# Exchanging even and odd chunks in the second RWKV head pair, so that the two pairs' recurrence products lie on opposite halves of the array, and copying z and U with two engines

## The chip, the cores and the metric

The kernel runs on one core of a Trainium2 chip. The metric is the device time of one execution in microseconds; for several runs of one kernel the median is given. TensorE (PE) multiplies; VectorE (DVE), ScalarE (ACT) and GpSimd (POOL) do the rest of the arithmetic; SyncE (SP) only issues DMA transfers here. Each engine takes its instructions in the order in which they are written and waits on semaphores for the others.

## The reference, cut to what matters

Two layers of a decoder trunk, 512 tokens, width 1024, batch 1, all in float32. Each layer adds three sub-layers to the residual: a token mixer, a cross-attention into 256 memory tokens, and a SwiGLU feed-forward network. The mixer projects its normalised input once, gives the columns to four groups of heads, and multiplies their joined outputs by `w_out`.

```python
y = concatenate([rglru_group(p_a, ...), retention_group(p_b, ...),
                 rwkv7_group(p_c, ...), ssd_group(p_d, ...)])
x = x + y @ w_out[l]
x = x + memory_cross_attention(...)
x = x + swiglu(...)
```

The change lies in the RWKV-7 group, which has 4 heads of 64 channels and a state of 64 x 64 for each head. Token by token it is

```python
def step(state, inp):                   # state (heads, v, k)
    r_t, w_t, k_t, v_t, kk_t, a_t = inp
    sa = einsum('bhvk,bhk->bhv', state, -kk_t)
    state = (state * w_t[:, :, None, :] + sa[..., None] * (kk_t * a_t)[:, :, None, :]
             + v_t[..., None] * k_t[:, :, None, :])
    return state, einsum('bhvk,bhk->bhv', state, r_t)
```

## The kernel before, in words

**A planner sets the order.** The kernel doesn't write its instructions straight into the program. Every operation is recorded as an `Op` with an engine, an estimated duration from `cost()` (line 376) and its dependences (`record()`, line 302). `order()` (line 428) then builds a list schedule: at each turn it takes, over all engines, the operation that can start first by these estimates; among equals of one engine it looks at a class (dense projection passes yield to group work), at whether TensorE would have to change its tile shape, and at the length of the path behind the operation. `issue()` (line 552) writes the operations in that order, so every instruction of the trace has line 564, and a group of instructions is known by its tiles. A name such as `b<-z,s 64*64 64x64` means: output in a tile of kind b, weights from a tile of kind z, data from a tile of kind s, weights of 64 rows by 64 columns, output of 64 x 64. The kinds are pools: `a` and `b` are PSUM banks (a for dense projections, b for the rest), `s` are 512 columns of SBUF, `q` 128 columns, `z` 256 columns, `t` small vectors, `u`, `v` and `w` the stages of a weight block.

**Dense projections.** A weight block of 1024 x 128 is loaded by DMA to `u`, cast by ScalarE to its high part `v` (a CAST of 128 x 1024), and VectorE subtracts to get the low part `w`. Three passes over 512 tokens (`a<-s,v`, `a<-s,v`, `a<-s,w`) make one product in split precision. These passes are most of TensorE's work, and the planner lays the small products of the four groups between them. A product of plain float32 operands shows as two passes in the trace, each with its own weight load.

**RWKV, prepared by `rwkv_pair` (line 1126).** Two heads make a pair (i = 0, 1) of 128 channels. The 512 tokens are 8 chunks of 64. Chunks 2q and 2q + 1 share a block of 128 token rows, so an even chunk (e = 0) and an odd one (e = 1) lie in different 64-row halves. `ar` holds four slots of 64 columns for each q: y, z, z, y (`a4[:, :, 1:3]` is for z, `a4[:, :, 0:4:3]` for y); `bk` holds the keys in the same manner. Their products, multiplied by the triangular mask `rwa`, are the tiles `at[hf, o]` (half of the sequence hf, head o of the pair). Their inner 128 columns go to a scratch `nd` in DRAM, 4 DMAs for each pair (line 1195).

**The solve, `rwkv_solve` (line 1212).** GpSimd inverts the unit triangles in blocks of 32, all chunks and heads side by side: `n<-nd` brings them in, 62 products and sums follow, and the results go out to scratch (`fd<-s`, `fd<-n`) and come back as tiles (`s<-fd`, 16 DMAs for each of two results). `rwkv_whole` (line 1260) then merges the blocks of 32 into inverses of 64: 16 products, a masked copy by VectorE (two `s<-b,cst` operations), 16 products more. Its products are the `b<-s,s 64*64` passes; neighbouring ones take e = 0 and e = 1 in turn, which are the two diagonal quarters of the array.

**The recurrence, `rwkv_scan` (line 1282).** Eight steps c, one for each chunk. In each step, for both pairs and both heads (`po`, four products in a group):

- z: `zb[rw, oc(i, o)] += at[...][:, zcol].T @ u` (weights 128 x 64), behind the product with the state `st[i]`; `z` is copied out of PSUM by VectorE (64 x 256);
- U: `ub[rw, oc(i, o)] = Rs[i].T-product with z` (`b<-z,s 64*64`), copied to `u` by ScalarE (64 x 256);
- the new state: one full product for each pair, two operations on VectorE;
- y: `zb[ry, oc(i, o)] += at[...][:, ycol].T @ u` (weights 128 x 64), copied by ScalarE.

`rw` and `ry` are the two halves of the 128 rows, and both are set by e alone, so both pairs use the same half in a step. The order within a group is that of `po`, with i outside and o inside.

**Retention** shares VectorE and SP with it at that time. For each of four tiles it copies a projection, shifts it by 32 partitions with four DMAs (`s<-s`, 32 x 512), and multiplies the result by the rotary table (`s<-s,s` of 128 x 512, two operations in sequence).

Of the kernel before, what the change touches and what calls it, by code (L numbers as in the profile page):

```python
# [13 lines left out]
AF = mybir.ActivationFunctionType  # L14
ALU = mybir.AluOpType
# [68 lines left out]
def _constants():  # L84
# [25 lines left out]
    blocks["retg"] = g  # L110

    s = np.arange(HD)
    lt, le = s[:, None] < s[None, :], s[:, None] <= s[None, :]
    am = np.concatenate([le, lt, lt, le], 1)
    blocks["rwa"] = np.concatenate([am, am], 0).astype(np.float64)
    m = (s[:, None] // 32 == 1) & (s[None, :] // 32 == 0)
# [136 lines left out]
class Engine:  # L253
# [9 lines left out]
KINDS = {"s": (T, 71), "n": (1024, 1), "z": (256, 2), "t": (16, 64), "q": (P, 10), "u": (KD * P + 16, 3), "v": (KD * P + 16, 3), "w": (KD * P + 16, 3),  # L263
         "a": (T, 3), "b": (T, 5)}


class Sched:
# [108 lines left out]
    def cost(self, op, fn, out, ins):  # L376
# [12 lines left out]
        elif op.eng == "PE":  # L389
            op.lat = 200.0  # L390
            if fn == "transpose":
                op.dur = 85.0
                op.grid = "T"
            else:
                k, m, w = ins[0].shape[0], _free(ins[0]), _free(ins[1])
                op.grid = HD if k <= HD else P, HD if m <= HD else P
                if ins[0].ap.dtype == F32R:
                    op.dur = max(111.0, 6 + 0.4405 * w)
                else:

# [166 lines left out]
class Trunk:  # L567
# [558 lines left out]
    def rwkv_pair(self, l, i, lora, wa, k, r, v, nd):  # L1126
# [30 lines left out]
        V.tensor_tensor(k2, k2, k, op=ALU.mult)  # L1157
        ar, bk = {}, {}
        for hf in range(2):
            ar[hf] = self.S()  # L1160
# [5 lines left out]

            V.tensor_tensor(a4[:, :, 1:3, 1:], q4(kk)[:, :, :, 1:], q4(wi)[:, :, :, :HD - 1], op=ALU.mult)
            V.tensor_copy(a4[:, :, 1:3, 0:1], q4(kk)[:, :, :, 0:1])
            V.tensor_tensor(a4[:, :, 0:4:3], q4(r), q4(wi), op=ALU.mult)

            V.tensor_tensor(b4[:, :, 0:4:3], q4(k2), q4(wv), op=ALU.mult)
        wend = self.tiny()[:, :8]
        V.tensor_copy(wend, wi[:, HD - 1:T:HD])
        V.scalar_tensor_tensor(kk, kk, -0.5, wv, op0=ALU.mult, op1=ALU.mult)
        for hf in range(2):
            ts_ = slice(hf * 256, (hf + 1) * 256)
            q3 = lambda x: x[:, ts_].rearrange("p (q t) -> p q t", q=2)
            V.scalar_tensor_tensor(bk[hf].rearrange("p (q x) -> p q x", q=2)[:, :, HD:3 * HD], q3(ta), 1.0, q3(kk),
                                   op0=ALU.add, op1=ALU.mult)

        am = self.con("rwa")
        at, bt = {}, {}
        for hf in range(2):
            for o in range(2):
# [9 lines left out]
                n0 = 8 * i + 4 * hf + 2 * o  # L1194
                self.Q.dma_start(nd[:, n0:n0 + 2], t.rearrange("p (q x) -> p q x", q=2)[:, :, HD:3 * HD])

# [7 lines left out]
        for hf in range(2):  # L1204
# [3 lines left out]
            bt[hf] = self.S()  # L1208
            A.copy(bt[hf], b)
        return ar, at, bt, wend, k2, kk, v  # L1210

# [47 lines left out]

    def rwkv_whole(self, RT, at):  # L1260

# [4 lines left out]
        col = lambda c: slice((4 * c[0] + 2 * c[1] + c[2]) * HD, (4 * c[0] + 2 * c[1] + c[2] + 1) * HD)  # L1266
        zcol = lambda q, e: slice(q * 2 * P + (1 + e) * HD, q * 2 * P + (2 + e) * HD)
        b = self.bank()
        for c in cells:
            E.matmul(b[rows(c[3]), col(c)], at[c[0], c[1]][rows(c[3]), zcol(c[2], c[3])], TT[rows(c[3]), col(c)], start=True, stop=True)  # L1270
        x = self.S()
# [10 lines left out]
    def rwkv_scan(self, l, pairs, RT):  # L1282
# [4 lines left out]
        rows = self.rows  # L1287
        zcol = lambda q, e: slice(q * 2 * P + (1 + e) * HD, q * 2 * P + (2 + e) * HD)
        ycol = lambda q, e: slice(q * 2 * P + 3 * e * HD, q * 2 * P + (3 * e + 1) * HD)

        uv = {}
        for hf in range(2):
# [4 lines left out]
            for i in range(2):  # L1297
# [4 lines left out]
                for e in range(2):  # L1302
                    rw = rows(1 - e)
                    A.copy(uv[hf, e][rw, i], b[rw, 0:256].rearrange("p (q x) -> p q x", q=2))
        Rs = [self.rwkv_whole(RT[i], pairs[i][1]) for i in range(2)]
        st = [None, None]
        yt = [p[5] for p in pairs]
        for c in range(8):
            hf, qq, e, q = c // 4, c % 4 // 2, c % 2, c // 2
            rw, ry = rows(e), rows(1 - e)  # L1310
            ccol = slice((c % 4) * P, (c % 4 + 1) * P)
            u = uv[hf, e][:, :, qq]
            z = self.s.tile("z")
            zb, ub = self.bank(), self.bank()
            oc = lambda i, o: slice(i * P + o * HD, i * P + (o + 1) * HD)
            po = [(i, o) for i in range(2) for o in range(2)]
            if c:
# [20 lines left out]
            for i, o in po:  # L1338
                E.matmul(zb[ry, oc(i, o)], pairs[i][1][hf, o][:, ycol(qq, e)], u[:, i, o * HD:(o + 1) * HD], start=(c == 0), stop=True, skip_group_check=True)
            for i in range(2):  # L1340
                A.copy(yt[i][ry, q * P:(q + 1) * P], zb[ry, i * P:(i + 1) * P])
        for i in range(2):
# [3 lines left out]
            for j in range(4):  # L1346
                E.transpose(b[:, j * P:(j + 1) * P], y[:, j * P:(j + 1) * P], ident)
            A.activation(y, b, AF.Identity, bias=self.par("rwkv_gn_b", l, i), scale=self.par("rwkv_gn_w", l, i))
            V.tensor_tensor(y, y, pairs[i][4], op=ALU.add)
# [364 lines left out]
```

## Time and profile before

| | |
|---|---|
| median of 3 runs | 1683.56 us (1681.34 to 1685.95) |
| profiled execution | 1683.98 us, span 1682.1 us |
| granted clock of TensorE, mean | 0.992 of full speed |
| TensorE busy | 1643.6 us (98%), 8344 passes |
| VectorE busy | 1015.1 us (60%), 1796 instructions |
| ScalarE busy | 633.2 us (38%), 966 instructions |
| GpSimd busy | 69.6 us (4%), 140 instructions |
| the chain that ended last | TensorE 91%, VectorE 4%, DMA 2%, ScalarE 2% |

The span is the profiler's view of one execution; the time is measured around it. Busy is the time in which an engine executes something, and passes of TensorE that overlap count once. The recurrence of the first layer runs from about 174 to 242 us, that of the second from about 1000 to 1060.

### The profile page before, as it was taken

How to read it: one execution, taken by the hardware profiler on the slowest of the kernel's cores; microseconds unless marked ns; L12 is line 12 of the kernel's file. 1: busy time of each engine (PE TensorE's matmuls, PEld its weight loads, DVE VectorE, ACT ScalarE, POOL GpSimd, SP SyncE). 2: the span in 40 equal slices, each digit the busy share in tenths (PEclk: the TensorE clock that was granted, in tenths of full speed). 3: DMA queues.
4: the chain of work that ended last, by engine and by line, in shares of the span. 5: the costliest groups of instructions: out<-in, count | busy, mean ns of one | idle time of the engine just before them, and what ended most of it. 6: DMA issues, size and time to landing. Idle time of an engine off the chain costs nothing.

```text
span 1682.1 us, 21417 instructions
## 1 busy us (share of the span) xinstructions
PE 1643.6 (98%) x8344; PEld 1344.0 (80%) x8344; DVE 1015.1 (60%) x1796; ACT 633.2 (38%) x966; POOL 69.6 (4%) x140
## 2 busy tenths in 40 slices
PE   7998999999999999999999989999999999999997
PEld 7786778888788888888888867888888888888886
DVE  8867689666564545533477666986655655554333
ACT  7433246444442322322354332554444323232221
POOL 0043000000000000000000700000000000000001
PEclk9999999999999999999999999999999999999998
DMA  9345112632323333333453431145233333333331
GB/s 287 103 101 126 26 45 81 189 94 66 97 88 99 89 100 90 95 104 114 131 175 101 107 83 45 51 126 162 64 88 88 100 89 99 93 96 94 92 97 57
DMA packets 312900, 169.48 MB, mean 101 GB/s; under 512 B 35936, under 2 KB 300384, under 8 KB 312672
## 3 DMA queue, kind: packets, MB, share of 16 engines
q1 hardware_dynamic: 312800, 168.12, 34.8%
q8 instruction: 66, 1.08, 0.3%
q14 instruction: 34, 0.28, 0.1%
HBM read 156.56 MB, written 9.44 MB: 99 GB/s over the span
## 4 chain that ended last, share of the span: by engine, by line
PE 91%; DVE 4%; DMA 2%; ACT 2%; SPq 1%; issue 1%; DVEq 0%; ACTq 0%
PE a L564 81%; PE b L564 9%; DVE s L564 2%; ACT s L564 1%; DMA s<-s 1%; DVE w L564 1%; SPq L564 1%; ACT v L564 1%; DMA s<-in_lora_dram 0%; DMA s<-fd 0%; DMA s<-in_memT_dram 0%; DVE q L564 0%; DVE t L564 0%; DVEq L1710 0%; DVE z L564 0%
## 5 line engine op out<-in xcount | busy, mean ns | idle before, releaser
L564 PE MATMUL a<-s,v 128*128 128x512 f32 (+1 forms) x4012 | 1234.0, 388 | 7.6 <-ACT s L564 5.9
L564 PEld LDWEIGHTS a<-s,v 128*128 128x128 f32 x4012 | 743.8, 189 | 168.2 <-ACT s L564 6.5
L564 PE MATMUL a<-s,w 128*128 128x512 f32 (+1 forms) x2006 | 777.2, 387 | 0.5 <-DVE w L564 0.5
L564 ACT CAST v<-u 128x1024 fp32r<-128x1024 f32 (+3 forms) x275 | 282.4, 1027 | 673.6 <-PE a L564 384.4
L564 PEld LDWEIGHTS a<-s,w 128*128 128x128 f32 x2006 | 378.8, 189 | 80.0 <-issue 0.9
L564 DVE TENSOR_TENSOR w<-u,v 128x1024 fp32r<-128x1024 f32 (+3 forms) x275 | 329.2, 1198 | 169.5 <-ACT v L564 168.8
L564 DVE TENSOR_TENSOR s<-a,s 128x512 f32<-128x512 f32 (+1 forms) x132 | 90.5, 689 | 264.1 <-PE a L564 244.9
L564 ACT ACTIVATE s<-s 128x512 f32<-128x512 f32 (+3 forms) x233 | 144.7, 628 | 111.9 <-DVE s L564 107.3
L564 PE MATMUL b<-s,s 64*64 64x64 f32 (+8 forms) x1268 | 146.0, 275 | 14.8 <-DVE s L564 9.2
L564 DVE TENSOR_TENSOR s<-s,s 128x512 f32<-128x512 f32 (+4 forms) x223 | 139.9, 636 | 30.8 <-DMA s<-s 16.2
L564 PEld LDWEIGHTS b<-s,s 128*128 128x128 f32 (+3 forms) x1268 | 120.9, 171 | 42.9 <-issue 17.3
L564 DVE SCALAR_TENSOR_TENSOR s<-s,s 128x512 f32<-128x512 f32 (+2 forms) x164 | 110.0, 676 | 8.3 <-ACT s L564 7.6
L564 DVE TENSOR_TENSOR s<-s,a 128x512 f32<-128x512 f32 (+1 forms) x49 | 33.2, 677 | 91.8 <-PE a L564 91.8
L564 PE MATMUL a<-v,s 128*128 128x260 f32 (+1 forms) x256 | 67.4, 344 | 0.0
L564 ACT COPY s<-b 64x256 f32<-64x256 f32 (+3 forms) x92 | 30.4, 354 | 80.2 <-PE b L564 74.8
L564 DVE SCALAR_TENSOR_TENSOR s<-s,prm,s 128x512 fp32r<-128x512 f32 (+3 forms) x78 | 52.8, 695 | 4.3 <-ACT s L564 4.2
L564 PE MATMUL b<-cst,s 128*128 128x128 f32 (+2 forms) x312 | 47.9, 266 | 2.3 <-ACT s L564 1.3
L564 PEld LDWEIGHTS a<-v,s 128*128 128x128 f32 x256 | 44.2, 188 | 5.6
L564 PEld LDWEIGHTS b<-cst,s 128*128 128x128 f32 x312 | 38.8, 159 | 11.5 <-DVE s L564 3.9
L564 DVE SCALAR_TENSOR_TENSOR s<-a,prm,s 128x511 f32<-128x511 f32 (+2 forms) x64 | 47.3, 740 | 0.7
L564 ACT CAST s<-s 128x512 fp32r<-128x512 f32 x48 | 29.2, 620 | 45.4 <-DVE s L564 40.4
L564 PE MATMUL a<-w,s 128*128 128x512 f32 (+1 forms) x128 | 43.4, 339 | 0.0
(92 smaller groups left out, 665.8 us busy)
## 6 DMA issues: line engine op xcount, KB each, us to landing
u<-in_ffn_w_in_dram SPq DMA_DIRECT2D x88, 512.0 KB, 3.7
u<-in_w_in_dram SPq DMA_DIRECT2D x52, 512.0 KB, 3.9
u<-in_ffn_w_out_dram SPq DMA_DIRECT2D x32, 512.0 KB, 3.7
u<-in_mem_wv_dram SPq DMA_DIRECT2D x16, 512.0 KB, 3.5
u<-in_w_out_dram SPq DMA_DIRECT2D x16, 512.0 KB, 3.8
u<-in_mem_wq_dram SPq DMA_DIRECT2D x16, 512.0 KB, 3.7
u<-in_mem_wo_dram SPq DMA_DIRECT2D x16, 512.0 KB, 3.7
u<-in_mem_wk_dram SPq DMA_DIRECT2D x13, 512.0 KB, 4.0
```

The source lines that it names most:

```text
L564: op.fn(*[real(x) for x in op.args], **{k: real(x) for k, x in op.kw.items()})
```

## The change: chunks of pair 1 exchanged, and two copies in place of one

For pair i = 1 the four slots of `ar`, `bk` and `at` hold z, y, y, z in place of y, z, z, y; the mask `rwa` gets 128 columns more and is read from a shifted start. In `rwkv_scan`, `rw` and `ry` become pairs, so that pair 1 uses the half that pair 0 doesn't. `po` runs over o outside and i inside, so that neighbours in a group belong to different pairs. The z tile becomes a `quarter()`; pair 0's part is copied by VectorE and pair 1's by ScalarE, and for U the other way round. The values v of pair 1 are written with their chunks exchanged, the inner columns of `at` go out in two pieces, and the last activation of pair 1 puts the chunks back. In `cost()`, the estimated duration of a product with at most 64 rows or columns of weights is halved, and with it the whole order is planned anew.

```diff
-KINDS = {"s": (T, 71), "n": (1024, 1), "z": (256, 2), "t": (16, 64), "q": (P, 10), ...
+KINDS = {"s": (T, 71), "n": (1024, 1), "t": (16, 64), "q": (P, 14), ...
...
+                if min(k, m) <= HD:
+
+                    op.dur /= 2
...
+        zs, ys = (slice(0, 4, 3), slice(1, 3)) if i else (slice(1, 3), slice(0, 4, 3))
-            V.tensor_tensor(a4[:, :, 1:3, 1:], q4(kk)[:, :, :, 1:], q4(wi)[:, :, :, :HD - 1], op=ALU.mult)
+            V.tensor_tensor(a4[:, :, zs, 1:], q4(kk)[:, :, :, 1:], q4(wi)[:, :, :, :HD - 1], op=ALU.mult)
...
+            for n, x in ((HD, 0), (HD, 3 * HD)) if i else ((P, HD),):
+                t0 = P - n if x > HD else 0
+                V.scalar_tensor_tensor(b3[:, :, x:x + n], q3(ta)[:, :, t0:t0 + n], 1.0, q3(kk)[:, :, t0:t0 + n], op0=ALU.add, op1=ALU.mult)
...
-                self.Q.dma_start(nd[:, n0:n0 + 2], t.rearrange("p (q x) -> p q x", q=2)[:, :, HD:3 * HD])
+                t4 = t.rearrange("p (q x) -> p q x", q=2)
+                if i == 0:
+                    self.Q.dma_start(nd[:, n0:n0 + 2], t4[:, :, HD:3 * HD])
+                else:
+                    for e, x in ((0, 3 * HD), (1, 0)):
+                        self.Q.dma_start(nd[:, n0:n0 + 2, e * HD:(e + 1) * HD], t4[:, :, x:x + HD])
...
+            for e in range(2):
+                A.copy(v2.rearrange("p (q e t) -> p q e t", e=2, t=HD)[:, :, e], v.rearrange("p (q e t) -> p q e t", e=2, t=HD)[:, :, 1 - e])
...
+    def zcol(i, q, j):
+
+        x = 4 * q + (3 * j if i else 1 + j)
+        return slice(x * HD, (x + 1) * HD)
+
+    def ycol(self, i, q, j):
+        return self.zcol(1 - i, q, j)
...
-            rw, ry = rows(e), rows(1 - e)
+            rw, ry = (rows(e), rows(1 - e)), (rows(1 - e), rows(e))
-            z = self.s.tile("z")
+            z = self.quarter()
-            po = [(i, o) for i in range(2) for o in range(2)]
+            po = [(i, o) for o in range(2) for i in range(2)]
...
-                E.matmul(zb[rw, oc(i, o)], pairs[i][1][hf, o][:, zcol(qq, e)], u[:, i, o * HD:(o + 1) * HD], start=(c == 0), stop=True, skip_group_check=True)
-            V.tensor_copy(z[rw], zb[rw, 0:2 * P])
+                E.matmul(zb[rw[i], oc(i, o)], pairs[i][1][hf, o][:, self.zcol(i, qq, e)], u[:, i, hd(o)], start=(c == 0), stop=True, skip_group_check=True)
+            V.tensor_copy(z[rw[0]], zb[rw[0], 0:P])
+            A.copy(z[rw[1]], zb[rw[1], P:2 * P])
-                E.matmul(ub[rw, oc(i, o)], Rs[i][rw, n * HD:(n + 1) * HD], z[rw, oc(i, o)], start=True, stop=True)
-            A.copy(u[rw], ub[rw, 0:2 * P].rearrange("p (i x) -> p i x", i=2))
+                E.matmul(ub[rw[i], oc(i, o)], Rs[i][rw[i], n * HD:(n + 1) * HD], z[rw[i], hd(o)], start=True, stop=True)
+            A.copy(u[rw[0], 0], ub[rw[0], 0:P])
+            V.tensor_copy(u[rw[1], 1], ub[rw[1], P:2 * P])
```

On TensorE, the first step of the recurrence in layer 0: before, the U group (`b0<-z0`) takes both heads of pair 0 (`s49`), then both of pair 1 (`s58`).

```order
L564 MATMUL b1_1566_1864<-cst_74,s8_1453_1508 128x128
L564 MATMUL b0_967_1871<-z0_966_1861,s49_850_1619 64x64 x2
L564 MATMUL b0_967_1871<-z0_966_1861,s58_855_1624 64x64 x2
L564 MATMUL a0_1745_1724<-s52_115_587,v1_1743_1564 128x512
L564 MATMUL a0_1745_1724<-s41_114_535,w1_1744_1580 128x512
```

After, the z group (`b3<-s48`) and the U group (`b2<-q0`) of the same step; `s39` and `s38` are the inverses of pair 0 and pair 1.

```order
L569 MATMUL b3_970_1920<-s48_880_1670,s12_562_903 64x64
L569 MATMUL b3_970_1920<-s48_880_1670,s50_740_1138 64x64
L569 MATMUL b3_970_1920<-s48_880_1670,s33_568_907 64x64
L569 MATMUL b3_970_1920<-s48_880_1670,s51_747_1144 64x64
L569 MATMUL a1_1805_1776<-s46_117_565,v2_1803_1616 128x512
L569 MATMUL a1_1805_1776<-s56_118_597,v2_1803_1616 128x512
L569 MATMUL a1_1805_1776<-s46_117_565,w2_1804_1630 128x512
L569 MATMUL b2_976_1933<-q0_974_1927,s39_858_1662 64x64
L569 MATMUL b2_976_1933<-q0_974_1927,s38_863_1667 64x64
L569 MATMUL b2_976_1933<-q0_974_1927,s39_858_1662 64x64
L569 MATMUL b2_976_1933<-q0_974_1927,s38_863_1667 64x64
```

The products of the two pairs now take turns.

On SP, the return of the solve's result in layer 0, before: `fd` goes out, retention's shifts of one tile (`s_1700`) are spread around the 16 loads `s_862` to `s_855`, and those of the next tile (`s_1735`) follow.

```order
L564 DMA fd_86<-s_782_1087 2048x1x16 x2
L564 DMA fd_85<-n_774_1164 1024x1x32 x2
L564 DMA s_1700_1645<-s_1699_1637 32x512 x2
L564 DMA u_2048_1655<-in_w_in_dram 128x8x128
L564 DMA s_1700_1645<-s_1699_1637 32x512
L564 DMA s_862_1603<-fd_86 32x8x32 x4
L564 DMA s_867_1614<-fd_86 32x8x32 x4
L564 DMA s_850_1619<-fd_85 32x8x32 x4
L564 DMA s_855_1624<-fd_85 32x8x32
L564 DMA u_2089_1753<-in_w_in_dram 128x8x128
L564 DMA s_855_1624<-fd_85 32x8x32 x3
L564 DMA s_1700_1645<-s_1699_1637 32x512
```

After, the same place; the tiles of retention are `s_1725` and `s_1760` here, the loads `s_870` to `s_863`.

```order
L569 DMA s_1725_1634<-s_1724_1627 32x512 x2
L569 DMA u_2073_1642<-in_w_in_dram 128x8x128
L569 DMA s_1725_1634<-s_1724_1627 32x512 x2
L569 DMA fd_85<-s_790_1061 2048x1x16 x2
L569 DMA fd_84<-n_782_1230 1024x1x32 x2
L569 DMA s_1760_1702<-s_1759_1694 32x512 x2
L569 DMA u_2114_1715<-in_w_in_dram 128x8x128
L569 DMA s_1760_1702<-s_1759_1694 32x512 x2
L569 DMA s_870_1654<-fd_85 32x8x32 x4
L569 DMA s_875_1658<-fd_85 32x8x32 x4
L569 DMA s_858_1662<-fd_84 32x8x32 x4
L569 DMA s_863_1667<-fd_84 32x8x32
```

All four shifts of each of the two tiles now stand ahead of the 16 loads.

## Rows read from the trace of the kernel before

**Rows 1.** The page, its first part: busy time and share of each engine.
```profile
PE 1643.6 (98%) x8344; PEld 1344.0 (80%) x8344; DVE 1015.1 (60%) x1796; ACT 633.2 (38%) x966; POOL 69.6 (4%) x140
```

**Rows 2.** TensorE's groups by shape: busy us, mean ns of one, idle before.
```profile
L564 PE MATMUL b<-s,s 128*64 128x64 f32 x256 | 22.8, 234 | 0.0
...
L564 PE MATMUL b<-z,s 64*64 64x64 f32 x128 | 10.8, 224 | 0.0
```

**Rows 3.** TensorE in order of time: start us, us, shape, passes in a row.
```profile
179.03 1.64 PE L564 MATMUL b<-s,s 128*128 128x128 f32 x14
180.42 0.47 PE L564 MATMUL a<-s,v 128*128 128x512 f32 x1
180.82 0.66 PE L564 MATMUL b<-s,s 128*64 128x128 f32 x8
181.41 0.67 PE L564 MATMUL b<-z,s 64*64 64x64 f32 x8
182.02 0.50 PE L564 MATMUL a<-s,v 128*128 128x512 f32 x1
...
195.07 0.68 PE L564 MATMUL b<-s,s 128*64 128x64 f32 x8
195.68 0.73 PE L564 MATMUL a<-s,v 128*128 128x512 f32 x2
```

**Rows 4.** TensorE in order of time, the merging of the solve's blocks.
```profile
159.92 1.02 PE L564 MATMUL b<-s,s 64*64 64x64 f32 x26
160.88 0.50 PE L564 MATMUL a<-s,v 128*128 128x512 f32 x1
```

**Rows 5.** TensorE in order of time, behind idle stretches (in brackets, with the releaser).
```profile
40.22 0.63 PE L564 MATMUL a<-s,v 128*128 128x512 f32 x1 [1.44 <-DVE s L564]
...
167.20 1.64 PE L564 MATMUL b<-s,s 64*64 64x64 f32 x24 [4.18 <-DVE s L564]
...
982.67 0.29 PE L564 MATMUL b<-s,s 64*64 64x64 f32 x2 [1.13 <-DMA s<-fd]
...
993.71 1.72 PE L564 MATMUL b<-s,s 64*64 64x64 f32 x26 [4.43 <-DVE s L564]
```

**Rows 6.** Stretches: length, busy us of PE, PEld, DVE, ACT, POOL, PEclk, DMA share, GB/s.
```profile
40.40:43.80 3.40, 3.40 (x9) 2.19 (x9) 3.40 (x6) 1.67 (x4) 0.00 (x0) 0.50 0.96 336
167.20:173.50 6.30, 6.30 (x58) 5.33 (x59) 3.10 (x5) 0.00 (x0) 0.00 (x0) 0.50 0.09 21
993.70:999.60 5.90, 5.89 (x57) 4.93 (x58) 3.10 (x5) 0.00 (x0) 0.00 (x0) 0.50 0.07 17
1020.00:1060.00 40.00, 38.58 (x287) 30.60 (x287) 26.98 (x74) 10.63 (x26) 0.00 (x0) 1.00 0.16 45
```

**Rows 7.** VectorE in order of time, ahead of the two long idle stretches' ends.
```profile
164.75 1.42 DVE L564 TENSOR_TENSOR s<-s,s 128x512 f32<-128x512 f32 x2 [4.53 <-DMA s<-s]
...
991.14 1.42 DVE L564 TENSOR_TENSOR s<-s,s 128x512 f32<-128x512 f32 x2 [4.41 <-DMA s<-s]
```

**Rows 8.** SP's DMA issues in order of time, layer 0.
```profile
95.11 2.15 SPq L564 DMA_DIRECT2D nd<-s  x4
...
151.96 7.49 SPq L564 DMA_DIRECT2D s<-fd  x13
```

**Rows 9.** GpSimd in order of time, the last operation of layer 0's solve.
```profile
141.73 0.22 POOL L564 TENSOR_TENSOR s<-s,n 128x16 f32<-128x16 f32 x1
```

**Rows 10.** The tile fd: time from a DMA's issue to its landing.
```profile
DMA to landing us min/median/max: 1.8/2.8/6.4
```

**Rows 11.** VectorE and ScalarE in order of time: the copies of z and of U.
```profile
180.34 0.42 DVE L564 COPY z<-b 64x256 f32<-64x256 f32 x1
...
182.12 0.37 ACT L564 COPY s<-b 64x256 f32<-64x256 f32 x1 [4.24 <-PE b L564]
```

**Rows 12.** The page, its fifth part: the split of the weights.
```profile
L564 ACT CAST v<-u 128x1024 fp32r<-128x1024 f32 (+3 forms) x275 | 282.4, 1027 | 673.6 <-PE a L564 384.4
...
L564 DVE TENSOR_TENSOR w<-u,v 128x1024 fp32r<-128x1024 f32 (+3 forms) x275 | 329.2, 1198 | 169.5 <-ACT v L564 168.8
```

More of the change, by code (lines that the diff above doesn't have):

```diff
@@ L114, in _constants @@
     am = np.concatenate([le, lt, lt, le], 1)
+    am = np.concatenate([am, am[:, :2 * HD]], 1)
     blocks["rwa"] = np.concatenate([am, am], 0).astype(np.float64)
@@ L260, in __getattr__ @@
         return lambda *a, **k: self.sched.record(self.eng, getattr(self.real, fn), fn, a, k)
-KINDS = {"s": (T, 71), "n": (1024, 1), "z": (256, 2), "t": (16, 64), "q": (P, 10), "u": (KD * P + 16, 3), "v": (KD * P + 16, 3), "w": (KD * P + 16, 3),
+KINDS = {"s": (T, 71), "n": (1024, 1), "t": (16, 64), "q": (P, 14), "u": (KD * P + 16, 3), "v": (KD * P + 16, 3), "w": (KD * P + 16, 3),
          "a": (T, 3), "b": (T, 5)}
@@ L1165, in rwkv_pair @@
             q4 = lambda x: x[:, ts_].rearrange("p (q e t) -> p q e t", q=2, e=2)
-            V.tensor_tensor(a4[:, :, 1:3, 1:], q4(kk)[:, :, :, 1:], q4(wi)[:, :, :, :HD - 1], op=ALU.mult)
-            V.tensor_copy(a4[:, :, 1:3, 0:1], q4(kk)[:, :, :, 0:1])
-            V.tensor_tensor(a4[:, :, 0:4:3], q4(r), q4(wi), op=ALU.mult)
-            V.tensor_tensor(b4[:, :, 0:4:3], q4(k2), q4(wv), op=ALU.mult)
+            V.tensor_tensor(a4[:, :, zs, 1:], q4(kk)[:, :, :, 1:], q4(wi)[:, :, :, :HD - 1], op=ALU.mult)
+            V.tensor_copy(a4[:, :, zs, 0:1], q4(kk)[:, :, :, 0:1])
+            V.tensor_tensor(a4[:, :, ys], q4(r), q4(wi), op=ALU.mult)
+            V.tensor_tensor(b4[:, :, ys], q4(k2), q4(wv), op=ALU.mult)
         wend = self.tiny()[:, :8]
@@ L1177, in rwkv_pair @@
             q3 = lambda x: x[:, ts_].rearrange("p (q t) -> p q t", q=2)
-            V.scalar_tensor_tensor(bk[hf].rearrange("p (q x) -> p q x", q=2)[:, :, HD:3 * HD], q3(ta), 1.0, q3(kk),
-                                   op0=ALU.add, op1=ALU.mult)
-        am = self.con("rwa")
+            b3 = bk[hf].rearrange("p (q x) -> p q x", q=2)
+            for n, x in ((HD, 0), (HD, 3 * HD)) if i else ((P, HD),):
+                t0 = P - n if x > HD else 0
+                V.scalar_tensor_tensor(b3[:, :, x:x + n], q3(ta)[:, :, t0:t0 + n], 1.0, q3(kk)[:, :, t0:t0 + n], op0=ALU.add, op1=ALU.mult)
+        am = self.con("rwa")[:, 2 * HD * i:2 * HD * i + 4 * HD]
         at, bt = {}, {}
@@ L1209, in rwkv_pair @@
             A.copy(bt[hf], b)
+        if i:
+            v2 = self.S()
+            for e in range(2):
+                A.copy(v2.rearrange("p (q e t) -> p q e t", e=2, t=HD)[:, :, e], v.rearrange("p (q e t) -> p q e t", e=2, t=HD)[:, :, 1 - e])
+            v = v2
         return ar, at, bt, wend, k2, kk, v
@@ L1258, in rows, with rwkv_whole @@
         return slice(HD, P) if e == 0 else slice(0, HD)
-    def rwkv_whole(self, RT, at):
+    @staticmethod
+    def zcol(i, q, j):
[3 more added lines that the diff above has]
+        return self.zcol(1 - i, q, j)
+    def rwkv_whole(self, i, RT, at):
         V, E = self.V, self.E
@@ L1266, in rwkv_whole @@
         col = lambda c: slice((4 * c[0] + 2 * c[1] + c[2]) * HD, (4 * c[0] + 2 * c[1] + c[2] + 1) * HD)
-        zcol = lambda q, e: slice(q * 2 * P + (1 + e) * HD, q * 2 * P + (2 + e) * HD)
         b = self.bank()
         for c in cells:
-            E.matmul(b[rows(c[3]), col(c)], at[c[0], c[1]][rows(c[3]), zcol(c[2], c[3])], TT[rows(c[3]), col(c)], start=True, stop=True)
+            E.matmul(b[rows(c[3]), col(c)], at[c[0], c[1]][rows(c[3]), self.zcol(i, c[2], c[3] ^ i)], TT[rows(c[3]), col(c)], start=True, stop=True)
         x = self.S()
@@ L1287, in rwkv_scan @@
         rows = self.rows
-        zcol = lambda q, e: slice(q * 2 * P + (1 + e) * HD, q * 2 * P + (2 + e) * HD)
-        ycol = lambda q, e: slice(q * 2 * P + 3 * e * HD, q * 2 * P + (3 * e + 1) * HD)
         uv = {}
@@ L1302, in rwkv_scan @@
                 for e in range(2):
-                    rw = rows(1 - e)
+                    rw = rows(1 - e ^ i)
                     A.copy(uv[hf, e][rw, i], b[rw, 0:256].rearrange("p (q x) -> p q x", q=2))
-        Rs = [self.rwkv_whole(RT[i], pairs[i][1]) for i in range(2)]
+        Rs = [self.rwkv_whole(i, RT[i], pairs[i][1]) for i in range(2)]
         st = [None, None]
@@ L1309, in rwkv_scan @@
             hf, qq, e, q = c // 4, c % 4 // 2, c % 2, c // 2
-            rw, ry = rows(e), rows(1 - e)
+            rw, ry = (rows(e), rows(1 - e)), (rows(1 - e), rows(e))
             ccol = slice((c % 4) * P, (c % 4 + 1) * P)
             u = uv[hf, e][:, :, qq]
-            z = self.s.tile("z")
+            z = self.quarter()
             zb, ub = self.bank(), self.bank()
             oc = lambda i, o: slice(i * P + o * HD, i * P + (o + 1) * HD)
-            po = [(i, o) for i in range(2) for o in range(2)]
+            hd = lambda o: slice(o * HD, (o + 1) * HD)
+            po = [(i, o) for o in range(2) for i in range(2)]
             if c:
@@ L1338, in rwkv_scan @@
             for i, o in po:
-                E.matmul(zb[ry, oc(i, o)], pairs[i][1][hf, o][:, ycol(qq, e)], u[:, i, o * HD:(o + 1) * HD], start=(c == 0), stop=True, skip_group_check=True)
+                E.matmul(zb[ry[i], oc(i, o)], pairs[i][1][hf, o][:, self.ycol(i, qq, e)], u[:, i, hd(o)], start=(c == 0), stop=True, skip_group_check=True)
             for i in range(2):
-                A.copy(yt[i][ry, q * P:(q + 1) * P], zb[ry, i * P:(i + 1) * P])
+                A.copy(yt[i][ry[i], q * P:(q + 1) * P], zb[ry[i], i * P:(i + 1) * P])
         for i in range(2):
@@ L1347, in rwkv_scan @@
                 E.transpose(b[:, j * P:(j + 1) * P], y[:, j * P:(j + 1) * P], ident)
-            A.activation(y, b, AF.Identity, bias=self.par("rwkv_gn_b", l, i), scale=self.par("rwkv_gn_w", l, i))
+            by_two = lambda x: x.rearrange("p (q e t) -> p q e t", e=2, t=HD)
+            for yo, bo in ((by_two(y)[:, :, e], by_two(b)[:, :, 1 - e]) for e in range(2)) if i else ((y, b),):
+                A.activation(yo, bo, AF.Identity, bias=self.par("rwkv_gn_b", l, i), scale=self.par("rwkv_gn_w", l, i))
             V.tensor_tensor(y, y, pairs[i][4], op=ALU.add)
```

## The prediction

> **What bounds the kernel now.** I read the busy shares first, then TensorE's groups by shape, TensorE's instructions in order of time around the recurrence, the waits in front of them, the stretches by granted clock, and last the queues that release the longest waits. The page's first part shows TensorE busy for 1643.6 of 1682.1 us, VectorE for 60% and ScalarE for 38% [rows 1]. So a change saves time in two ways only: TensorE's instruction stream becomes shorter, or one of its few idle or half-clock stretches goes. A change loses time when TensorE is made to wait.
>
> The stream that the change touches is small: 256 passes for z and y (weights of 128 rows by 64 columns) and 128 for U (64 by 64) [rows 2]; a product in fp32 is two passes. Every recurrence step has three groups of 8 passes (z, U, y), there are 8 steps in a layer and two layers: 48 groups.
>
> **What one group costs now, and what it costs with alternating halves.** The group of 8 U passes at 181.41 takes 0.67 us from its first start to its last end, and the dense pass behind it starts 0.61 us after the group [rows 3]. One pass by itself lasts 0.22 on the mean [rows 2], and passes overlap. With 7 intervals, (0.67 - 0.22) / 7 = 0.064 us per pass. The group at 195.07, with weights of 128 rows by 64 columns, takes 0.68: the same 0.065. In both, all 8 passes use one half of the array.
>
> The kernel has a place where 64-wide passes alternate between halves already: the merging of the solve's blocks, whose neighbours lie on the two diagonal quarters. There 26 passes take 1.02 us, and the next starts 0.96 us after the first [rows 4]: (1.02 - 0.22) / 25 = 0.032 us per pass. That is exactly U's new situation, since pair 0 and pair 1 will lie on opposite diagonal quarters and the order by o, then i, makes neighbours alternate. For z and y the halves differ in columns only, with all 128 rows used by both. The nearest row is the group at 180.82, 8 passes over 128 columns of data that write alternate halves of the output: (0.66 - 0.22) / 7 = 0.063 us, against (1.64 - 0.22) / 13 = 0.109 for 14 full-array passes over as many columns, at 179.03 [rows 3] (both a little high, since a pass over 128 columns is longer than 0.22). So column halves overlap there too, by a factor of 1.7. For z and y with 64 columns I take U's 0.032, as a factor of 2.
>
> The saving is 7 x (0.064 - 0.032) = 0.22 us for a group, and 48 x 0.22 = 10.6 us. The planner's order takes some back. In the changed order the 32 groups with 128 rows stand in 39 runs, so about 7 are cut in two by a dense pass, as the four passes ahead of the U group shown above. A cut costs one more entry into and exit from small passes: 0.61 for 8 passes at 0.064 leaves 0.61 - 0.51 = 0.10, and one overlap of 0.03 is lost; the dense pass ahead of such a group is spaced by 0.40 (180.42 to 180.82) where dense passes follow each other at 0.73 - 0.50 = 0.23 (two at 195.68 take 0.73, one at 182.02 takes 0.50) [rows 3]. That makes 0.17 to 0.3 for a cut; I take 0.23, 1.6 us. Term one: **-9 us**, with bounds from -2 (only U overlaps) to -11 (no cut costs anything).
>
> The Trainium skill, page "TensorE: Matmul & The Clock Gate", section "Part 3: Packing small matmuls — row/col tiling", says that a weight load overlaps running matmuls only when its row group differs. By that rule z and y, which differ in columns alone, would gain nothing, and term one would be 16 x 0.22 - 1.6 = -2 us. The row at 180.82 speaks against it: those passes share all rows, each brings its own weights [rows 3], and they still come at 0.063 us.
>
> **What is added.** VectorE gets 20 instructions more and ScalarE 22: the copies of z and U are 64x128 on two engines in place of one 64x256 each, which took 0.42 (VectorE) and 0.37 (ScalarE) [rows 11]; four more products of 64 columns for bk; two copies a layer that exchange chunks of v, and one more normalising activation a layer. I cost them at nothing. What hides them is TensorE's own work: between 1020 and 1060 us, in the recurrence, TensorE is busy for 38.58 of 40 us, VectorE for 26.98 and ScalarE for 10.63 [rows 6]. Without cover, 42 x 0.2 to 0.4 us would be 8 to 17 us. Splitting a copy in two also shortens what the next product waits for, so the bound is open below nothing too; I take 0.
>
> **The solve's return path, where something is moved.** Pair 1's triangles now go out by 8 DMAs in place of 4, since the two 64-halves aren't neighbours any more. Four issues took 2.15 us [rows 8], so the solve's input is complete 2.15 us later. In layer 0 pair 1's products are also ordered behind some 35 more dense passes of 260 columns, about 4.2 us at 0.12 each (0.23 x 260 / 512). GpSimd is done at 141.95 in the kernel before [rows 9], and so at about 148.3 now.
>
> Who waits for that? There are two long stalls on TensorE, 4.18 us before 167.20 and 4.43 before 993.71, and one of 1.13 on the solve's data at 982.67 [rows 5]: 9.7 us. The two long ones aren't the solve's own time. VectorE works in order, and it stood idle for 4.53 us, until a DMA of the rotary pass had landed, at 164.75, and for 4.41 at 991.14 [rows 7]; the masked product that TensorE waits for is queued behind these. The rotary DMA in its turn stood behind 16 loads of the solve's result on the queue of SP (13 of them 7.49 us) [rows 8]. In the changed order of layer 0 the rotary DMAs of that tile and of the next stand ahead of these loads, so VectorE isn't blocked there. What is late next is the solve itself: the loads began 10.0 us behind GpSimd's end (151.96 - 141.95) and will begin at 148.3 + 10.0 + 0.6 = 158.9; the first four, at 0.58 each and landing 2.8 us after issue [rows 10], are there at 158.9 + 1.7 + 2.8 = 163.4. TensorE ran dry at 163.0 before (167.20 - 4.18), with two stretches of 26 products (2.0 us) just ahead that now come behind the wait, so it is dry at 161: a wait of 2.5, and one of about 0.8 for the second pair. In layer 1 the same walk, with 2.15 us of delay and two more rotary DMAs ahead of some loads, gives a wait of 2.7 for the first block and 1.2 for the first z copy, which stands behind the next tile's two rotary products on VectorE. Together 7.2 in place of 9.7: -2.5 us.
>
> Each long stall was also paid a second time. Behind them TensorE ran at a granted clock of 0.50, from 167.2 to 173.5 and from 993.7 to 999.6 [rows 6]; this is the lower of its two levels, and costs half of 6.3 + 5.9, 6.1 us. After an idle time of only 1.44 us, at 40.22, the low level held for 3.4 us, which costs 1.7 [rows 5, 6]. With waits of 2.5 to 2.7 I expect one such shorter stretch in each layer: 3.4 in place of 6.1, -2.7 us. Term two is **-5 us**; its bounds are +6 (the waits as long as before, with one more) and -15.8 (none left: 9.7 + 6.1).
>
> **Sum.** The profiled execution took 1683.98 us (span 1682.1), within 0.5 us of the median of 1683.56. 1683.98 - 9 - 5 = **1670 us**, 0.8% faster. A measurement of this kernel can tell about 0.3%, 5 us, from no change.
>
> **Rivals.** (A) Column halves don't overlap when the weights have 128 rows and the data only 64 columns, a combination that no row shows. Then term one is -2 and the time 1684 - 2 - 5 = 1677. For it: the short passes leave little to hide a weight load behind. Against it: the group at 180.82.
>
> (B) The stalls come back at full length. The solve ends 6 us later in layer 0, and it has little slack: if VectorE or SP put one more rotary pass in front, both stalls are 4 us and more again and the low clock holds as long as before. Term two is then between 0 and +4, and the time 1675 to 1679, middle 1677. Against it: the rotary DMAs stand ahead in the order.
>
> (C) The recurrence becomes the bound, which makes the kernel slower. Each step now waits for both engines twice, z for a copy on ScalarE and U for one on VectorE besides the former two. Those engines work in order, and the split of the weights puts 1.03 us casts on ScalarE and 1.20 us subtractions on VectorE [rows 12]. If both stand in front of a copy in each step, that is 2.2 us, of which the dense passes between a step's products hide perhaps 1 (my estimate): 16 x 1.25 = 20 us, 1690. From 14 / 16 = 0.9 us of exposed wait in a step it decides the sign. Against it: TensorE idles for only 1.4 us of 40 in the recurrence [rows 6].
>
> (D) The stalls vanish altogether, because the shorter waits are filled with dense passes: 1684 - 9 - 15.8 = 1659.
>
> That the change doesn't do what it says, so that neighbours don't alternate, I leave out: the order shows them alternating.
>
> **Chances.** Forecast 0.55 (own range 1665 to 1676), A 0.12, B 0.13, C 0.08, D 0.12. Faster by over 0.3% (below 1678.5): 0.53 + 0.06 + 0.08 + 0.12 = 0.79. Within 0.3%: 0.15, from A, B and the edges. Slower: 0.06, nearly all C. The range from 1659 to 1682 leaves out half of D, C, and the ends of A and B, under 2 in 10.
>
> **What would show it.** In the profile after: groups of 8 z, U and y passes of about 0.45 us from first start to last end (0.66 for z and y alone would be A); waits before the first merging products of 2 to 3 us, ended by a DMA of the solve's result and not by VectorE; half-clock stretches near 3.4 us; TensorE's idle time between recurrence steps as before (if it grows by 1 us a step, C). The forecast is wrong if the groups stay at 0.67, or if idle time elsewhere, from a list that is planned anew, eats more than 9 us.

## The result, and the profile after

The changed kernel takes 1656.97 us (median of 5 runs, 1656.22 to 1658.63) against 1684.28 us for the kernel before on the same chip: a ratio of 0.9838, 95% interval 0.9825 to 0.9851. That is 27 us, where 14 were forecast, and below the low end of the range. The profiled execution is 1656.97 us with a span of 1655.2; before it was 1682.1.

The groups became as short as forecast. TensorE's groups by shape in the changed kernel (busy us, mean ns of one, idle before), to be held against [rows 2]:

```profile
L569 PE MATMUL b<-s,s 128*64 128x64 f32 x256 | 16.7, 235 | 1.9 <-DVE s L569 1.9
...
L569 PE MATMUL b<-q,s 64*64 64x64 f32 x128 | 8.0, 237 | 0.0
```

and the first step of the recurrence in order of time, against [rows 3]:

```profile
173.68 0.45 PE L569 MATMUL b<-s,s 128*64 128x64 f32 x8
174.06 0.73 PE L569 MATMUL a<-s,v 128*128 128x512 f32 x2
174.63 0.40 PE L569 MATMUL a<-s,w 128*128 128x512 f32 x1
174.96 0.45 PE L569 MATMUL b<-q,s 64*64 64x64 f32 x8
```

Both kinds of group go from 0.67 or 0.68 to 0.45 us, and the next instruction starts 0.38 us after the group's first in place of 0.61. Column halves overlap as well as diagonal quarters: (0.45 - 0.22) / 7 = 0.033 us a pass.

The rest of the gain is waiting that went. In place of the stalls of 4.18 and 4.43 us [rows 5] stand these two waits, the second of them ahead of the first z group and not of the merging:

```profile
161.93 2.64 PE L569 MATMUL b<-s,s 64*64 64x64 f32 x26 [1.69 <-DMA s<-fd]
...
980.01 0.45 PE L569 MATMUL b<-s,s 128*64 128x64 f32 x8 [1.93 <-DVE s L569]
```

and the half-clock stretches behind them 3.4 us each, against 6.3 and 5.9 in [rows 6]:

```profile
162.30:165.70 3.40, 3.40 (x33) 2.62 (x34) 3.13 (x6) 0.59 (x1) 0.00 (x0) 0.50 0.32 49
981.50:984.90 3.40, 3.40 (x16) 2.35 (x15) 3.05 (x8) 1.94 (x3) 0.00 (x0) 0.50 0.00 0
```

VectorE's waits tell why. First the row of before, then the row of after (total us, times, longest):

```profile
DVE s L564 <- DMA s<-s: 16.2, 7, 4.5
```

```profile
DVE s L569 <- DMA s<-s: 2.5, 1, 2.5
```

These are the waits for retention's shifts. Before, the merging's masked copies (`s<-b,cst`) are queued behind them; after, the one wait that is left stands behind these copies.

For an account I added up, over all 8344 passes, the time from each pass's start to the next one's, and took out idle time and one half of what ran at the low clock:

| us | before | after | difference |
|---|---|---|---|
| passes with 64 columns of weights (z, U, y, merging, SSD halves) | 44.3 | 35.1 | -9.2 |
| all other passes | 1591.0 | 1587.5 | -3.5 |
| TensorE idle between passes | 23.4 | 13.9 | -9.5 |
| cost of the low clock | 7.8 | 3.1 | -4.7 |
| together | 1666.5 | 1639.7 | -26.8 |

Of the -9.2 us, 8.3 are in z, U and y; of the -4.7 us, 1.7 are the stretch at 40.40 [rows 6], which the trace after doesn't have.

### The profile page after: what moved, and what is told of

It is laid out like the page before. It is cut to its first block, busy times and chain, and to the rows that moved or that the text cites. A ratio compares the mean times of both kernels' runs of the same rounds, so it can differ in the third digit from the quotient of the medians.

```text
span 1655.2 us, 21468 instructions
## 1 busy us (share of the span) xinstructions
PE 1626.0 (98%) x8344; PEld 1329.1 (80%) x8344; DVE 1015.0 (61%) x1816; ACT 640.0 (39%) x988; POOL 67.1 (4%) x140
## 4 chain that ended last, share of the span: by engine, by line
PE 92%; DVE 2%; DMA 2%; ACT 1%; SPq 1%; issue 0%; DVEq 0%; ACTq 0%
PE a L569 84%; PE b L569 9%; DVE s L569 2%; SPq L569 1%; ACT s L569 1%; DMA u<-in_mem_wk_dram 1%; DMA u<-in_w_in_dram 1%; DVE w L569 0%; DMA s<-fd 0%; DVE t L569 0%; ACT v L569 0%; DMA s<-in_memT_dram 0%; DMA s<-s 0%; ACT n L569 0%; DVEq L1742 0%
## 5 line engine op out<-in xcount | busy, mean ns | idle before, releaser
L569 PE MATMUL b<-s,s 128*64 128x64 f32 (+8 forms) x1268 | 134.6, 270 | 6.2 <-DVE s L569 3.5
L569 PEld LDWEIGHTS b<-s,s 128*128 128x128 f32 (+3 forms) x1268 | 111.5, 167 | 34.4 <-issue 9.1
L569 DVE TENSOR_TENSOR s<-s,a 128x512 f32<-128x512 f32 (+1 forms) x49 | 33.2, 677 | 92.5 <-PE a L569 92.5
L569 ACT COPY s<-b 64x128 f32<-64x128 f32 (+3 forms) x92 | 29.9, 335 | 63.3 <-PE b L569 47.4
L569 PEld LDWEIGHTS a<-v,s 128*128 128x128 f32 x256 | 44.3, 188 | 5.7
```

The lines of the kernel that those rows point to most:

```text
L569: op.fn(*[real(x) for x in op.args], **{k: real(x) for k, x in op.kw.items()})
```

## The experiments

Three things change at once: the layout (exchanged halves, turns, two copiers), the halved price in `cost()`, and by it the order of everything. In the expectations, theory P says that the waits went by the new plan, R that they went by a shorter recurrence; S that a low price helps because it leaves slack, T because it is nearer the truth; D that the stalls hang on SP's queue. "Half" in the table is the first row of the account, "shifts" the time in which VectorE waited for retention's shifts.

| kernel | layout | price | shifts on | us | ratio, 95% interval | half | other | idle | low clock | shifts |
|---|---|---|---|---|---|---|---|---|---|---|
| before | old | 1 | SP | 1684.28 | | 44.3 | 1591.0 | 23.4 | 7.8 | 16.2 |
| after | new | 1/2 | SP | 1656.97 | 0.9838 (0.9825-0.9851) | 35.1 | 1587.5 | 13.9 | 3.1 | 2.5 |
| e1 | old | 1/2 | SP | 1659.57 | 0.9841 (0.9820-0.9862) | 43.4 | 1582.9 | 14.3 | 1.6 | 7.9 |
| e2 | new | 1 | SP | 1686.32 | 0.9998 (0.9984-1.0011) | 34.7 | 1590.5 | 31.3 | 14.1 | 18.5 |
| e3 | new, no turns | 1/2 | SP | 1657.72 | 0.9835 (0.9814-0.9856) | 33.2 | 1588.4 | 14.4 | 6.4 | 3.2 |
| e4 | new, one copier | 1/2 | SP | 1661.18 | 0.9852 (0.9831-0.9872) | 33.5 | 1589.6 | 16.6 | 5.0 | 3.6 |
| e5 | old | 1/2 for 64x64 | SP | 1670.82 | 0.9909 (0.9890-0.9928) | 43.1 | 1590.8 | 15.3 | 3.4 | 12.6 |
| e6 | old | 1/2 for the others | SP | 1677.82 | 0.9947 (0.9930-0.9965) | 43.3 | 1586.3 | 20.8 | 11.8 | 14.5 |
| e10 | old, allowance 600 | 1 | SP | 1679.32 | 0.9959 (0.9944-0.9974) | 44.4 | 1589.6 | 22.7 | 6.0 | 12.7 |
| e7 | new | 1/3 | SP | 1648.72 | 0.9776 (0.9755-0.9797) | 33.8 | 1585.1 | 11.5 | 1.5 | 3.3 |
| b1 | new | 1/4 | SP | 1666.37 | 0.9886 (0.9870-0.9901) | 33.8 | 1589.7 | 19.3 | 6.9 | 1.1 |
| e9 | old | 1 | ScalarE | 1666.99 | 0.9892 (0.9878-0.9906) | 44.9 | 1590.0 | 13.9 | 0.1 | 1.7 |
| e11 | new | 1 | ScalarE | 1669.81 | 0.9903 (0.9888-0.9919) | 37.6 | 1594.8 | 16.3 | 5.2 | 0.5 |
| a_rot | new | 1/2 | ScalarE | 1658.19 | 0.9829 (0.9806-0.9851) | 34.1 | 1589.8 | 14.8 | 1.6 | 1.1 |
| b2 | new | 1/3 | ScalarE | 1648.58 | 0.9783 (0.9769-0.9797) | 32.5 | 1588.1 | 9.6 | 1.6 | 8.2 |
| b3 | new | 1/2.5 | ScalarE | 1646.00 | 0.9759 (0.9737-0.9781) | 32.1 | 1584.8 | 11.0 | 0.0 | 2.8 |
| e12 | old | 1/3 | SP | 1665.47 | 0.9873 (0.9850-0.9896) | 43.8 | 1589.9 | 12.2 | 1.7 | 2.0 |
| e13 | old | 1/3 | ScalarE | 1660.82 | 0.9848 (0.9825-0.9872) | 43.8 | 1587.4 | 9.9 | 1.7 | 0.0 |

Ratios are to the kernel before in runs beside each; its medians were 1684.3 to 1686.1 us. The last five columns are from one profiled execution each; up to 3.4 us of "low clock" come from stretches near the start, between 23 and 47 us: the trace after has none of them, that of before has one and that of e11 two, and nothing here ties them to the edits.

**The price alone (e1) and the layout alone (e2).**

```diff
 # e1: the kernel before, plus
+                if min(k, m) <= HD:
+                    op.dur /= 2
 # e2: the changed kernel, minus these lines
```

> The kernel before with the planner's halved price for small products and nothing else: layout, copies and products as before, so all groups of z, U and y stay on one half and their passes at about 0.064 us. Theory P (planner): the waits and half-clock stretches went because the list was planned anew with the halved price; they go here too, so 1684 - 14 = 1670 us (1666 to 1674), TensorE idle for about 20 us or less in place of 29. Theory R (recurrence): the waits went because each step of the recurrence is shorter and its copies lie on two engines; then nothing goes here, 1682 to 1686 us, with the two stalls of over 4 us still there.

> The changed kernel with the planner's old price (no halving), so exchanged chunks, turns and two copiers, but a list planned with the old numbers. Theory P: only the overlap is left, 1684 - 9 = 1675 us (1672 to 1678), with stalls of about 4 us in front of the merging products and half-clock stretches of 6 us behind them. Theory R: 1656 to 1661 us, waits as in the changed kernel.

The price alone gives 26.6 of the 27.3 us, and the layout alone nothing. R falls. P names the right part, but both of its times miss: 1659.6 against 1670 and 1686.3 against 1675. In e1 the groups are still long:

```profile
178.69 0.68 PE L567 MATMUL b<-z,s 64*64 64x64 f32 x8
```

In e2 they are short (half 34.7), but the stalls are worse than before. VectorE and TensorE of e2 in layer 1:

```profile
994.21 1.42 DVE L566 TENSOR_TENSOR s<-s,s 128x512 f32<-128x512 f32 x2 [5.95 <-DMA s<-s]
995.55 0.75 DVE L566 TENSOR_TENSOR s<-b,cst 128x256 f32<-128x256 f32 x2
```

```profile
996.40 1.46 PE L566 MATMUL b<-s,s 64*64 64x64 f32 x22 [4.31 <-issue]
```

VectorE waits 5.95 us for a shift; the masked copy `s<-b,cst` is behind it, and TensorE's merging starts 0.1 us behind that copy's end (the trace names no releaser, "issue"). It is the stall of [rows 7] again. In the recurrence TensorE idles for 7.7 us here, counted from the first to the last U pass of each layer and summed over both, against 4.0 before and 0.2 after.

**Turns within a group (e3) and the copiers (e4).**

```diff
-            po = [(i, o) for o in range(2) for i in range(2)]            # e3
+            po = [(i, o) for i in range(2) for o in range(2)]
-            A.copy(z[rw[1]], zb[rw[1], P:2 * P])                         # e4
+            V.tensor_copy(z[rw[1]], zb[rw[1], P:2 * P])
-            V.tensor_copy(u[rw[1], 1], ub[rw[1], P:2 * P])
+            A.copy(u[rw[1], 1], ub[rw[1], P:2 * P])
```

> The changed kernel with the products of a group in the former sequence, pair outside and head inside, so that four passes of one half are followed by four of the other in place of taking turns. Both theories: groups of 8 take 0.60 to 0.67 us in place of 0.45, 48 x 0.15 to 0.22 = 7 to 11 us more, 1664 to 1668 us, if neighbours are what overlaps. If it is enough that a group uses both halves somewhere, the group stays at 0.45 and the time at 1657 us (1655 to 1659).

> The changed kernel with both copies of z on VectorE and both copies of U on ScalarE, as before the change, in place of one on each. Theory P: within 3 us of the changed kernel, 1655 to 1660 us. Theory R: the second copy in sequence adds 0.2 to 0.4 us twice in each of 16 steps, 6 to 13 us, 1663 to 1670 us.

Turns aren't needed. With four passes of one half written ahead of four of the other, the groups are as short (e3, TensorE in order of time):

```profile
176.91 0.46 PE L569 MATMUL b<-s,s 128*64 128x64 f32 x8
...
178.20 0.45 PE L569 MATMUL b<-q,s 64*64 64x64 f32 x8
```

One copier costs 4.2 us by the medians and 2.4 by the ratios, whose intervals overlap: between P and R, nearer to P. Its extra idle time isn't in the steps: the longest waits of e4 are 2.42 us at 162 and 2.93 at 984, ahead of the recurrence, as in the changed kernel.

**Why a low price helps: slack or truth (e10, e5, e6, e7, b1).**

```diff
-            lat = a.lat + (200.0 if data and b.eng == "PE" and b.cls == 1 else 0.0)   # e10
+            lat = a.lat + (600.0 if data and b.eng == "PE" and b.cls == 1 else 0.0)
+                if max(k, m) <= HD:                    # e5; e6: min(k, m) <= HD < max(k, m)
+                    op.dur /= 2
-                    op.dur /= 2                        # e7: by 3; b1: by 4
+                    op.dur /= 3
```

> The kernel before with its old prices, and one number of the planner changed: the allowance that it adds to a dependence of a TensorE product on another engine's result is 600 ns in place of 200. Layout, copies and products as before. Theory S (slack): the halved price helped because it lets the planner put more dense passes between a result and the product that waits for it, so that real delays are covered; then this number does it as well, with full prices: TensorE's idle time 15 us in place of 23 behind the start, one long half-clock stretch or none, 1660 to 1668 us. Theory T (truth): it helped because the halved price is nearer to what small products take; then nothing or little goes here, 1680 to 1688 us.

> The kernel before with the price halved for products of 64 x 64 alone (merging of the solve's blocks and U). Theory T: these are the products whose old price was too high where they alternate (merging: 0.064 us a product, old price 0.116), so most of the gain comes, 1660 to 1668 us. Theory S: a third of the 35 us by which the planned small work shrinks (11 of 35), so part of the gain, 1670 to 1680 us.

> The kernel before with the price halved for products with 64 rows or 64 columns but not both (z, y, the triangles and scores), whose old price was about right in this layout. Theory T: the plan gets worse or stays, 1680 to 1690 us. Theory S: two thirds of the shrinking (24 of 35 us), most of the gain, 1660 to 1670 us.

> The changed kernel with the price of small products divided by 3 in place of 2. Theory S: still more slack, no loss, 1652 to 1660 us. Theory T: further from the truth, waits or shape changes come back, 1662 to 1675 us.

> The changed kernel with the price of small products divided by 4. Theory S: slack is there already at 3, so 1646 to 1652 us. Theory T: worse than by 2, 1658 to 1675 us.

Neither theory holds. T falls with e7, which is further from the truth (0.039 us a product, where two passes at 0.033 take 0.066) and 8 us faster, and with e5, which came out in S's range. S falls with e10 and b1: 400 ns more allowance gave 5 us of the 17 to 25 expected, and dividing by 4 cost 18 us against dividing by 3. e6, at 1677.8, lies between the two. The table's last column sorts them better: all five kernels in which VectorE waited over 12 us for shifts (before, e2, e5, e6, e10) take 1670 us or more, the others less. In e10 the allowance didn't reach that wait (VectorE, then TensorE):

```profile
989.11 1.42 DVE L564 TENSOR_TENSOR s<-s,s 128x512 f32<-128x512 f32 x2 [4.87 <-DMA s<-s]
```

```profile
991.67 1.51 PE L564 MATMUL b<-s,s 64*64 64x64 f32 x22 [4.62 <-issue]
```

What sets these five apart is an order on VectorE. In both layers of each, a rotary product that waits 2.4 to 6.0 us for a late shift stands between the masked copies of the first and of the second pair. In the kernel before, layer 0, the first pair's copies are at 158.33, the rotary products at 164.75 [rows 7], and the second pair's copies behind them:

```profile
166.09 0.42 DVE L564 TENSOR_TENSOR s<-b,cst 128x256 f32<-128x256 f32 x1
```

In e1 the rotary products stand behind the second pair's copies (VectorE), though their four shifts still follow the 16 loads on SP:

```profile
164.89 0.76 DVE L567 TENSOR_TENSOR s<-b,cst 128x256 f32<-128x256 f32 x2 [2.57 <-DMA s<-fd]
...
167.71 1.42 DVE L567 TENSOR_TENSOR s<-s,s 128x512 f32<-128x512 f32 x2 [2.06 <-DMA s<-s]
```

```profile
163.78 2.42 SPq L567 DMA_DIRECT2D s<-s  x4
```

The same order stands in after, e3, e4, e7, e12 and b1: no wait for a shift comes between the two pairs' copies. No run exchanges the two on VectorE and leaves the rest, so that this is what the price does is read from the traces and not tested. Nor is it the whole condition: in b2 VectorE waits 4.30 and 3.85 us for a shift ahead of the second pair's copies, and TensorE, which has dense passes to run there, idles for 0.41 us at most.

**The queue itself (e9, e11).**

```diff
-                    self.Q.dma_start(s[o:o + 32], c[32 * b:32 * b + 32])     # retention
+                    self.A.dma_start(s[o:o + 32], c[32 * b:32 * b + 32])
```

> The kernel before, old prices and layout, with retention's four shifts of each tile issued on ScalarE's DMA queue in place of SP's, so that they don't stand behind the 16 loads of the solve's result. Theory D (a queue): the two long stalls come from VectorE waiting for a shift queued behind those loads; they go, with the half-clock stretches behind them: 1684 - 8.6 - 6 = 1669 us (1666 to 1673), and VectorE's waits of 4.5 us for the shift with them. Theory S alone (too little slack in general): the plan has no more slack than before, and 1680 to 1686 us.

> The changed kernel with the old price, and retention's shifts on ScalarE's queue. Against the run of the kernel before with the same edit this shows what exchanged halves and two copiers are worth at the old price where no long stall hides it. If the overlap is worth its 9 us: 1660 us (1657 to 1664), 9 less than that run. If TensorE gives it back as waits because a list with the old price has no slack: 1666 to 1672 us, the same as that run.

D holds. This one edit to the kernel before takes 18 us, with the old price and layout. The list is planned anew here too, but the first two columns of the account move by 1 us or less. VectorE's waits and the stretch that was a stall in [rows 5]:

```profile
DVE s L564 <- DMA s<-s: 1.7, 2, 0.9
```

```profile
163.00:167.20 4.20, 4.20 (x56) 3.40 (x55) 3.03 (x8) 0.00 (x0) 0.00 (x0) 1.00 0.46 121
```

TensorE is busy for all of 163.0 to 167.2, where it was idle for 4.18 us. Idle time falls from 23.4 to 13.9, exactly where the changed kernel has it, and the low clock from 7.8 to 0.1. But e11 shows that at the old price the layout gives nothing even so: half is 7.3 us less, other passes 4.8 more, idle 2.4 more, low clock 5.1 more (3.4 of it near the start, which isn't the layout's doing).

**What the layout is worth at a price of one third (e12, e13), and combinations (a_rot, b2, b3).** The edits are those above, on the old or the new layout.

> The kernel before (old layout, products on one half, one copier each) with the price of small products divided by 3. Against the changed kernel by 3 (1648.7) this shows what exchanged halves and two copiers are worth in a plan with slack. If TensorE's shorter groups count in full: 1657 to 1660 us, 9 to 11 more. If they are given back as in the runs at the old price: 1648 to 1653 us.

> The same with retention's shifts on ScalarE's queue, against the changed kernel by 3 with that edit (1648.6). Full worth: 1656 to 1659 us. Given back: 1647 to 1651 us.

> The changed kernel as it is (price halved) with retention's shifts on ScalarE's queue. Theory D: what is left of stalls in the changed kernel is one wait of 1.9 us in layer 1 behind such a shift and a half-clock stretch of 3.4 us (1.7 us); they go, 1657 - 3.6 = 1653 us (1651 to 1655). If the plan gives it back elsewhere: 1655 to 1660 us.

> The changed kernel with the price divided by 3 and retention's shifts on ScalarE's queue. Theory D and S together: only 1.1 us of waits are left around the merging, so within 3 us of the run by 3 without it: 1645 to 1650 us. If ScalarE's issues (about 0.5 us each, 16 a layer) delay the casts of the weights: 1652 to 1660 us.

> The changed kernel with the price divided by 2.5 and the shifts on ScalarE's queue. Theory S: between the runs by 2 and by 3, 1648 to 1653 us. If the time of a plan is a scatter that no price explains: anywhere from 1645 to 1668 us, as the run by 4 (1666) came out against the one by 3 (1649).

At one third the layout counts in full and more: 1665.5 to 1648.7 us with the shifts on SP, 1660.8 to 1648.6 on ScalarE. So it is worth 11 to 17 us there (by ratios and by medians); at one half 0.5 to 2.6 us, within the intervals; at the full price nothing (e2) or 2 to 3 us of loss (e9 to e11). e12 came out 5.5 us above the higher of its two ranges, and e13 1.8 us above. In all five pairs "half" shrinks by 7.3 to 11.3 us; what differs is how much the new plan gives back in the other columns. The queue adds nothing where VectorE's list already had the masked copies ahead of the rotary product that waits (after, e7). a_rot, at 1658.2, lies in its second range and not in D's: the wait of 1.93 us went, but waits of 1.98 and 1.30 us for the solve's data came. b3 is the fastest, 1646.0 us, below S's range, and beats both kernels.

That prices between 2.5 and 3 are best isn't shown as a rule; with 4, TensorE waited 3.39 us for the solve's data (b1):

```profile
162.35 0.30 PE L569 MATMUL b<-s,s 64*64 64x64 f32 x2 [3.39 <-DMA s<-fd]
```

## Why the prediction was wrong

**Term one, the overlap: right.** Forecast -9, measured -9.2 us in TensorE's stream, 8.3 of them in z, U and y. Rival A falls. The Trainium skill's sentence in "TensorE: Matmul & The Clock Gate" ("Part 3: Packing small matmuls — row/col tiling"), that a weight load overlaps running matmuls only when its row group differs, doesn't describe these passes: with all 128 rows shared they come at 0.033 us.

**The added copies: nothing, right in this plan.** In the recurrence TensorE idles for 0.2 us after and for 4.0 before, so rival C falls: no step became the bound. In e2's plan the same copies go with 7.7 us. e4 takes none of them out; it shows only what the second copier is worth.

**The solve's return: the walk was right in kind, too late in layer 0.** SP and GpSimd in order of time:

```profile
96.93 4.36 SPq L569 DMA_DIRECT2D nd<-s  x8
...
157.90 8.04 SPq L569 DMA_DIRECT2D s<-fd  x13
```

```profile
143.93 0.22 POOL L569 TENSOR_TENSOR s<-s,n 128x16 f32<-128x16 f32 x1
```

Eight issues take 4.36 us, 2.2 more than four [rows 8], as forecast. But GpSimd ends at 144.15 and not 148.3: the 4.2 us for later products of pair 1 weren't there. The loads begin at 157.90 (forecast 158.9), and that is luck: they come 13.8 us behind GpSimd's end in place of 10.6, since four shifts stand ahead of `fd` on SP, and the two errors nearly cancel. TensorE waits 1.69 and 0.19 us for them (forecast 2.5 and 0.8). In layer 1 the wait for the first block (2.7) isn't there at all, and the one ahead of the first z is 1.93 (1.2).

**Term two: the step that failed.** It was "Together 7.2 in place of 9.7: -2.5 us". The three waits that it counts went from 9.7 to 3.8 us (1.69, 0.19 and 1.93): -5.9. And it counted these alone of the 23.4 us of idle time and took the rest as fixed, since the kernel's other parts weren't changed; but a list that is planned anew moves those too: the rest fell by 3.6, and in the recurrence alone idle time fell from 4.0 to 0.2. In layer 1 I replaced a stall by waits from a walk whose times were each good to a microsecond or two, against slack of the same size. The term for the clock was right where I priced it: -2.7 forecast for the stretches behind the stalls, -3.0 measured; the other 1.7 us of the -4.7 are the stretch near the start. Rival D, at 1659, was nearest and had 0.12, but by its number alone: the stalls didn't vanish, 3.8 us of waits and 3.1 of low clock are left.

**What the sum left out.** The halved price had no term of its own. I read it as something that reorders SP's queue here and there; e1 shows that it gives 26.6 us by itself; in the account 15.3 of its 24.3 us are idle time and low clock, and 8.1 are other passes. e9 shows that 18 us hung on the shifts' place in SP's queue. In e1 the long stalls go with the shifts left there, and the trace has VectorE take the masked copies first. The stall was in front of me, in [rows 7, 8] and in the two orders. I used it to shorten two stalls and not to ask what the kernel would take without them. The other passes' -3.5 us had no term either, and where they come from isn't shown. They aren't fewer changes between weight shapes on TensorE: these are 196 before, 201 after and 177 in e1.

What stays open: why a plan with one price has less idle time elsewhere than one with another. Between neighbouring prices the runs differ by 3 to 18 us (with the shifts on ScalarE 1658 by 2, 1646 by 2.5, 1649 by 3; on SP 1649 by 3, 1666 by 4), and no number orders them.

## What to carry to other kernels

When a change touches the numbers of a scheduler, price the two separately, the new plan and the edit; run each alone, because here the edit's 9 us counted in full, hardly or not at all, depending on the plan. Before that, follow each long stall back through the in-order queues to the first thing that is late: here a DMA of 64 KB behind 16 others held VectorE, VectorE held TensorE, and the low clock made the bill longer. Moving it to another queue was worth 18 us by itself; a list in which the operation that waits stands behind the one that TensorE needs had 15 us less of idle time and low clock without that (e1).

## What the runs showed of the hardware that wasn't expected

Products on opposite halves overlap even when they aren't neighbours. In e3 the program has four passes of one half ahead of four of the other, and in the trace the passes start in pairs: 13 to 14 ns apart within a pair, and 45 to 94 ns from a pair to the next. On one half, in the kernel before, no pass of the groups at 181.41 and 195.07 starts less than 58 ns behind the last. That a pair is one pass of each half is inferred, as the trace doesn't name the half. 8 passes take 0.46 us as with turns; on one half they take 0.67. Column halves with all 128 rows in use behave in this as diagonal quarters do.
